# Where a branch is taken, where fetched rows are added, and how a weight row is repeated: three edits in a two-layer encoder kernel

## The chip, the cores and the metric

The kernel runs on one core of a Trainium2 chip. The metric is the device time of one execution in microseconds (us). Three runs of the kernel before gave 1431.76, 1432.56 and 1432.91 us; their median is 1432.56 us.

The names of the engines: PE is TensorE (matrix products; PEld are its weight loads), DVE is VectorE, ACT is ScalarE, POOL is GpSimd, SP is SyncE, which here only issues transfers. Each engine runs its own list of instructions in order; they meet by semaphores.

## The reference

A trunk of two layers over 256 tokens of width 1024, in float32:

```python
h = h + retention_mixer(rms_norm(h, mix_norm[0]), ...)
h = h + swiglu(rms_norm(h, ffn_norm[0]), ...)            # dense
h = h + fourier_mixer(rms_norm(h, mix_norm[1]), ...)
h = h + moe_swiglu(rms_norm(h, ffn_norm[1]), ...)        # top 2 of 8 experts
return rms_norm(h, final_norm)

def moe_swiglu(h, w_router, w_gate, w_up, w_down):
    logits = t @ w_router                                # t: 256 x 1024
    top_val, top_idx = lax.top_k(logits, 2)
    gates = sum(one_hot(top_idx) * softmax(top_val))
    for e in range(8):
        out = out + gates[:, e] * ((silu(t @ w_gate[e]) * (t @ w_up[e])) @ w_down[e])
```

An expert has 1024 x 3584 (gate, up) and 3584 x 1024 (down) weights. With 256 tokens that choose two experts each, an expert gets 64 tokens on average.

## The kernel before, in words

Three stages (retention, dense feed-forward, Fourier mixing) come first; from about 480 us on, the experts run. All three edits lie in the expert stage.

**Precision by splitting.** A float32 operand is split into a high and a low part; a product is the sum of three (`mm3`, lines 248 to 250: whi, wlo and whi again). So each weight tile that lands (`raw`, 1 MB, issued by SP at line 105) is cast to `whi` by ACT (line 131) and reduced to `wlo` by DVE (line 132), each in two halves. Three pairs of `whi`/`wlo` buffers rotate: ACT starts on tile i+2 once PE is through with tile i-1. Eleven `raw` buffers are filled ahead; a buffer is free for the next load when DVE has read it.

**Blocks.** An expert has 7 blocks of 512 hidden columns; there are 56 blocks, counted by `u`. A block is 6 weight tiles of 12 products each on PE: two of the gate, two of the up projection, and two of the down projection of the block before. Between the two gate tiles PE transposes the last block's hidden values (`t4`, line 294, tile `tr<-ident,hm`), which ACT and DVE split into `hth` and `htl` (lines 253 and 254). The hidden values are SiLU of the gate on ACT (line 1107) and its product with up on DVE (line 1111), both as `hm`. At the end of an expert its result goes to a table of rows `back` in DRAM (line 976).

**Small steps between.** A list `work` holds steps that are put between the products: one is taken in the middle of a block (during the first up tile), one at its end. `prep` gathers the tokens of the next two experts. `collect(c)` adds the rows that were fetched for token half c-1 to `X` on DVE (line 904) and then has POOL fetch those of half c by an indirect transfer from `back` (line 909). `final_parts(c)` splits `X` for the last sum (`xf`). `final_gain(hf)` repeats the 1024 final norm weights on all partitions by a product with a row of ones on PE and a copy on ACT (lines 1064 and 1065).

**The overflow branch.** Each expert has 128 slots. If an expert has more tokens, a branch after block 31 (`OVER_AT`) does the rest. The largest count is loaded into a register of each engine (line 1124) and compared (line 1129). In these inputs no expert overflows, so the body is skipped: each engine that has instructions in it jumps over them. The body uses the buffers of the main path (`tr`, two of `mm`, `acc2`, `acc3`), so what comes after the branch waits for the last user of such a buffer inside the body, and gets past when that engine has passed its branch.

The order of the work is written out by hand: instructions stand on each engine in the order in which the program issues them.

Of the kernel before, what the change touches and what calls it, by code (L numbers as in the profile page):

```python
# [11 lines left out]
AF = mybir.ActivationFunctionType  # L12
OP = mybir.AluOpType
PS = bass.MemoryType.PSUM

P = 128
D = 1024
S = 256
# [3 lines left out]
NE = 8  # L22
EPS = 1e-6
HALF = [slice(0, 512), slice(512, 1024)]


def cp(c):
    return slice(c * P, (c + 1) * P)
# [124 lines left out]
def body(nc, tc, a, out, upto=None):  # L153
    with ExitStack() as ctx:
# [6 lines left out]
        te, ve, se, ge = nc.tensor, nc.vector, nc.scalar, nc.gpsimd  # L161
# [53 lines left out]
        gb = gx[:, :D]  # L215
        xgs = [gx[:, D + 512 * i:D + 512 * (i + 1)] for i in range(2)]

        def gain_bcast(ap):
            nc.scalar.dma_start(gb, bcast_rows(ap, D))
# [8 lines left out]
        slot = const.tile([P, P], F32, name="slot")  # L228
        ones = const.tile([P, P], F32, name="ones")
# [11 lines left out]
        def mm(nm="mm"):  # L241
            return ps.tile([P, 512], F32, name=nm, tag="mm", bufs=3)
# [106 lines left out]
        with tc.tile_pool(name="pa", bufs=1) as pa:  # L349
# [43 lines left out]
            p = mm("g8")  # L393
# [171 lines left out]
            q = rope(proj({-1: [second], 0: [first]}, [acc(0), acc(1)]))  # L565
# [8 lines left out]
            q = rope(proj({0: [val(1, 0)], 1: [val(1, 1)], 2: [tg[0].step(0)], 3: [tg[0].step(1)]}))  # L574
# [29 lines left out]
        pt = Aligned(pt_.enter_context(tc.tile_pool(name="pt", bufs=1, side="right")))  # L604
# [4 lines left out]
        with tc.tile_pool(name="pb", bufs=1) as pb:  # L609
# [30 lines left out]
            for u in range(6):  # L640
# [21 lines left out]
                o = dense_h(u)  # L662
# [38 lines left out]
        with tc.tile_pool(name="pc", bufs=1) as pc:  # L701
# [70 lines left out]
            o1, mask, pos, m8 = (const.tile([P, 2, NE], F32, name=n) for n in ("o1", "mask", "pos", "m8"))  # L772
# [65 lines left out]
        with tc.tile_pool(name="pe", bufs=1) as pe, tc.tile_pool(name="dr", bufs=1, space=bass.MemoryType.DRAM) as dr:  # L838
# [61 lines left out]
            def collect(c):  # L900


                for j, t in got:
                    ve.tensor_add(X[:, c - 1], X[:, c - 1], t[:, j])  # L904
                got.clear()
                if c < 2:
                    t = pe.tile([P, 2, D], F32, name="yc", tag="y")
                    for j in range(2):
                        ge.indirect_dma_start(t[:, j], None, back,  # L909
                                              bass.IndirectOffsetOnAxis(at[:, 2 * j + c:2 * j + c + 1], 0))  # L910
                        got.append((j, t))
# [27 lines left out]
            work = list(prep(0))  # L939
            for f in work[:-1]:  # L940
                f()
            work = work[-1:]
# [66 lines left out]
            def overflow(sh, gl, pm, pmr, xe, pt, h, ht, w, gu, tr, y):  # L1009

                for e in range(NE):
                    for c in range(2):
                        ve.tensor_scalar(sh[:, c:c + 1], pos[:, c, e:e + 1], -float(P), None, op0=OP.add)
                        ve.tensor_scalar(pm[:, c], slot, sh[:, c:c + 1], mask[:, c, e:e + 1],
                                         op0=OP.is_equal, op1=OP.mult)
                    ve.tensor_copy(pmr, pm)
                    for q in range(2):
                        o = gu[q]
                        for i in range(4):
                            for c in range(2):  # L1020
                                te.matmul(o[:, cp(i)], nh[:, c, cp(4 * q + i)], pmr[:, c], start=c == 0, stop=False)
                                te.matmul(o[:, cp(i)], nl[:, c, cp(4 * q + i)], pmr[:, c], start=False, stop=c == 1)
                        ve.tensor_copy(xe[:, 4 * q:4 * q + 4], o.rearrange("p (i s) -> p i s", i=4))
                    for c in range(2):
                        te.transpose(tr[:, cp(c)], pm[:, c], ident)
                    ve.tensor_copy(pt, tr[:, :S])
                    for c in range(2):
                        te.matmul(tr[:, :NE + 1], pm[:, c], gts[:, c], start=c == 0, stop=c == 1)
                    ve.tensor_copy(gl, tr[:, :NE + 1])
                    rs, gt = gl[:, NE:], gl[:, e:e + 1]  # L1030
                    for b in range(FE // 512):
                        for o, n in zip(gu, ("moe_w_gate", "moe_w_up")):
                            for s in range(2):
                                wv = w.rearrange("p (k n) -> p k n", k=4)
                                nc.sync.dma_start(wv, cols(a[n][0, e], 512 * b, 512, 4 * s, 4))
                                for k in range(4):
                                    te.matmul(o, xe[:, 4 * s + k], wv[:, k], start=s == 0 and k == 0,
                                              stop=s == 1 and k == 3)
                        se.activation(h, gu[0], AF.Silu, scale=rs)
                        ve.scalar_tensor_tensor(h, gu[1], rs, h, op0=OP.mult, op1=OP.mult)  # L1040
                        for k in range(4):
                            te.transpose(tr[:, cp(k)], h[:, cp(k)], ident)
                        ve.tensor_copy(ht, tr)
                        for s in range(2):
                            wv = w.rearrange("p (k n) -> p k n", k=2)
                            nc.sync.dma_start(wv, cols(a["moe_w_down"][0, e], 0, D, 4 * b + 2 * s, 2))
                            for k in range(2):
                                for hf in range(2):
                                    te.matmul(y[hf], ht[:, cp(2 * s + k)], wv[:, k, HALF[hf]],
                                              start=b == 0 and s == 0 and k == 0,  # L1050
                                              stop=b == 6 and s == 1 and k == 1)
                    for hf in range(2):
                        ve.tensor_scalar(w[:, HALF[hf]], y[hf], gt, None, op0=OP.mult)
                    for c in range(2):
                        for hf in range(2):
                            o = gu[hf]
                            te.matmul(o, pt[:, cp(c)], w[:, HALF[hf]], start=True, stop=True)
                            x = X[:, c, HALF[hf]]
                            ve.tensor_add(x, x, o)

            def final_gain(hf):

                o = mm("gain")
                te.matmul(o, ones[:1], gb[:1, HALF[hf]], start=True, stop=True)  # L1064
                se.copy(gb[:, HALF[hf]], o)

            fin, of = {}, []

# [20 lines left out]
            for u in range(NU):  # L1089
                e, b = divmod(u, 7)  # L1090
                if b == 0 and e % 2 == 1 and e + 1 < NE:
                    work += list(prep(e + 1))
                if u == 2:
                    work.append(rows)
                if b == 1 and e == NE - 1:
                    work[:0] = [lambda c=c: collect(c) for c in range(3)]
                if u == OVER_AT + 3:
                    work += [lambda hf=hf: final_gain(hf) for hf in range(2)]
                if u == NU - 5:
                    work += [lambda c=c: final_parts(c) for c in range(2)]  # L1100
                for s, o in enumerate(moe_h(e)):
                    if s == 0 and u:
                        hidden_t(u - 1)
                    if s == 0 and not u:
                        work.pop(0)()
                hm = pe.tile([P, 512], F32, name="hm")
                se.activation(hm, o, AF.Silu, scale=RS[e])
                for s, o in enumerate(moe_h(e)):
                    if s == 0 and work:
                        work.pop(0)()  # L1110
                ve.scalar_tensor_tensor(hm, o, RS[e], hm, op0=OP.mult, op1=OP.mult)
                hms[u] = hm
                if u == NU - 1:
                    final_start(1)
                if u:
                    moe_down(u - 1, (lambda: hidden_t(NU - 1)) if u == NU - 1 else None)
                if work:
                    work.pop(0)()
                if u == NU - 2:
                    final_start(0)  # L1120
                if u == OVER_AT - 2:
                    counts()
                if u == OVER_AT - 1:
                    most = nc.values_load(cmi[0:1, 0:1])
                    tc.mark_branch_hint_location("over", most > P, engines=[te.engine, ve.engine, nc.sync.engine])
                if u == OVER_AT:
                    nc.scalar.dma_start(gb[:1], a["final_norm"].rearrange("(o d) -> o d", o=1))
                    ov = overflow_tiles()
                    with tc.If(most > P, label="over"):  # L1129
                        overflow(**ov)  # L1130
# [73 lines left out]
```

## Time and profile before

| | before |
|---|---|
| median of 3 runs | 1432.56 us |
| the profiled execution | 1431.94 us, of this the span from first to last instruction 1430.1 us |
| PE busy | 1405.9 us, 98% |
| DVE busy | 1164.9 us, 81% |
| ACT busy | 969.8 us, 68% |
| POOL busy | 70.2 us, 5% |
| mean granted clock of TensorE | 0.995 of full speed |
| transfers | 437.45 MB, in the expert stage about 350 to 390 GB/s |

Times in rows are microseconds from the start of the span. In a row of the timeline the first number is the start, the second the length (of all instructions merged in it; `x4` says how many), and in brackets stands how long the engine sat idle before, and what ended that. `PEq`, `DVEq` and `SPq` are the engines' sequencers, which handle branches and issue transfers.

### The profile page before, as it was taken

What the parts mean: (1) busy time and instruction counts of PE and PEld (TensorE: products, weight loads), DVE (VectorE), ACT (ScalarE), POOL (GpSimd) and SP (SyncE); (2) the same over time, 40 slices, a digit from 0 to 9 for tenths busy, and PEclk for the clock granted to TensorE, in tenths of its full rate; (3) what the DMA queues carried; (4) which work ended last, traced back from release to release, by engine and by line L of the source; (5) the groups of instructions that cost most, each with busy time, mean ns of one, the idle gap of its engine ahead of it and who ended that gap; (6) DMA issues with size and microseconds to landing.
All of it is one profiled execution on the core that took longest, in us unless ns stands there. A gap on an engine that the chain in (4) does not pass through costs nothing. (4 is left out here: it accounts for less than half of the span.)

```text
span 1430.1 us, 17313 instructions
## 1 busy us (share of the span) xinstructions
PE 1405.9 (98%) x6533; PEld 1166.7 (82%) x6533; DVE 1164.9 (81%) x1201; ACT 969.8 (68%) x1120; POOL 70.2 (5%) x109
## 2 busy tenths in 40 slices
PE   7999999999999999999999999999999999999997
PEld 6888878888888888888888888887878888888786
DVE  6866666545577999989999988998988898999996
ACT  5544446444455777777877777787777778778775
POOL 8400000000001000000000000000000000001000
PEclk9999999999999999999999999999999999999999
DMA  8646539755536989999999999999999999999990
GB/s 288 213 154 205 177 132 375 251 179 200 181 120 243 385 302 358 371 356 340 334 394 393 386 361 364 362 347 390 348 373 361 356 373 366 393 383 346 395 347 30
DMA packets 186700, 437.45 MB, mean 306 GB/s; under 512 B 8161, under 2 KB 10993, under 8 KB 186610
## 3 DMA queue, kind: packets, MB, share of 16 engines
q1 hardware_dynamic: 181424, 426.27, 81.7%
q10 hardware_dynamic: 4610, 7.92, 1.5%
q0 software_dynamic: 576, 2.10, 0.4%
q8 instruction: 52, 0.85, 0.2%
q14 instruction: 38, 0.31, 0.1%
HBM read 431.54 MB, written 4.72 MB: 305 GB/s over the span
## 5 line engine op out<-in xcount | busy, mean ns | idle before, releaser
L132 DVE TENSOR_TENSOR wlo<-raw,whi 128x1024 fp32r<-128x1024 f32 (+1 forms) x789 | 923.5, 1219 | 148.3 <-ACT whi L131 139.9
L131 ACT CAST whi<-raw 128x1024 fp32r<-128x1024 f32 (+1 forms) x789 | 786.1, 1047 | 200.7 <-PE acc L250 106.3
L248 PE MATMUL mm<-whi,xe 128*128 128x512 f32 x896 | 355.1, 396 | 0.3 <-PEq L1129 0.3
L250 PE MATMUL mm<-whi,xe 128*128 128x512 f32 x896 | 349.6, 390 | 0.0
L249 PE MATMUL mm<-wlo,xe 128*128 128x512 f32 x896 | 349.2, 390 | 0.0
L249 PE MATMUL acc<-wlo,hth 128*128 128x512 f32 x528 | 206.3, 391 | 2.3 <-DVE wlo L132 2.3
L248 PE MATMUL acc<-whi,hth 128*128 128x512 f32 x528 | 206.2, 391 | 0.0
L250 PE MATMUL acc<-whi,htl 128*128 128x512 f32 x528 | 206.1, 390 | 0.0
L250 PEld LDWEIGHTS mm<-whi,xe 128*128 128x128 f32 x896 | 168.2, 188 | 36.1
L248 PEld LDWEIGHTS mm<-whi,xe 128*128 128x128 f32 x896 | 168.4, 188 | 34.9 <-issue 2.2
L249 PEld LDWEIGHTS mm<-wlo,xe 128*128 128x128 f32 x896 | 168.5, 188 | 32.9
L248 PE MATMUL mm<-whi,nhi 128*128 128x512 f32 (+1 forms) x352 | 135.6, 385 | 0.0
L250 PE MATMUL mm<-whi,nlo 128*128 128x512 f32 (+1 forms) x352 | 133.9, 380 | 0.0
L249 PE MATMUL mm<-wlo,nhi 128*128 128x512 f32 (+1 forms) x352 | 133.7, 380 | 0.0
L249 PEld LDWEIGHTS acc<-wlo,hth 128*128 128x128 f32 x528 | 99.5, 188 | 23.3 <-DVE wlo L132 2.8
L250 PEld LDWEIGHTS acc<-whi,htl 128*128 128x128 f32 x528 | 99.5, 188 | 20.7
L248 PEld LDWEIGHTS acc<-whi,hth 128*128 128x128 f32 x528 | 99.6, 189 | 20.6
L253 ACT CAST hth<-tr 128x512 fp32r<-128x512 f32 (+1 forms) x67 | 38.9, 581 | 84.8 <-PE tr L294 84.8
L250 PEld LDWEIGHTS mm<-whi,nlo 128*128 128x128 f32 x352 | 66.2, 188 | 12.9
L249 PEld LDWEIGHTS mm<-wlo,nhi 128*128 128x128 f32 x352 | 66.3, 188 | 11.8
L248 PEld LDWEIGHTS mm<-whi,nhi 128*128 128x128 f32 x352 | 66.3, 188 | 11.9
L254 DVE TENSOR_TENSOR htl<-tr,hth 128x512 fp32r<-128x512 f32 (+1 forms) x67 | 45.7, 682 | 33.5 <-ACT hth L253 33.5
(291 smaller groups left out, 992.6 us busy)
## 6 DMA issues: line engine op xcount, KB each, us to landing
raw<-in_moe_w_gate SPq DMA_DIRECT2D x110, 1024.0 KB, 7.6
raw<-in_moe_w_down SPq DMA_DIRECT2D x108, 1024.0 KB, 7.6
raw<-in_moe_w_up SPq DMA_DIRECT2D x105, 1024.0 KB, 7.3
raw<-in_ret_w_in SPq DMA_DIRECT2D x23, 1024.0 KB, 5.2
raw<-in_dense_w_gate SPq DMA_DIRECT2D x11, 1024.0 KB, 5.3
raw<-in_dense_w_up SPq DMA_DIRECT2D x11, 1024.0 KB, 8.8
raw<-in_dense_w_down SPq DMA_DIRECT2D x11, 1024.0 KB, 6.6
raw<-in_ret_w_out SPq DMA_DIRECT2D x8, 1024.0 KB, 4.9
```

The source lines that it names most:

```text
L131: self.nc.scalar.copy(hi[sl], t[sl])
L132: self.nc.vector.tensor_sub(lo[sl], t[sl], hi[sl].bitcast(F32))
L248: te.matmul(o, lh, rh, start=first, stop=False)
L249: te.matmul(o, lh, rl, start=False, stop=False)
L250: te.matmul(o, ll, rh, start=False, stop=last)
L253: se.copy(hi, src)
L254: ve.tensor_sub(lo, src, hi.bitcast(F32))
```

## The change

There are three parts.

1. The body of the overflow branch uses no DVE. What DVE did there is done by ACT (copies, casts and scalings) and POOL (the choice of slots, products of two tiles, the additions to `X`). The hint that names the engines of the branch lists ACT in place of DVE.
2. `collect(0)`, `collect(1)` and `collect(2)` are put in the list at blocks 50, 51 and 52 (b = 1, 2 and 3 of the last expert); all three were put there at block 50.
3. The final norm's weights are read by one transfer that repeats the row on all 128 partitions (`gain_bcast`, 512 KB, issued by ACT at block 34). Before, 4 KB were loaded just before the branch, and `final_gain` did the rest at block 34.

```diff
                 for e in range(NE):
                     for c in range(2):
-                        ve.tensor_scalar(sh[:, c:c + 1], pos[:, c, e:e + 1], -float(P), None, op0=OP.add)
-                        ve.tensor_scalar(pm[:, c], slot, sh[:, c:c + 1], mask[:, c, e:e + 1],
+                        ge.tensor_scalar(sh[:, c:c + 1], pos[:, c, e:e + 1], -float(P), None, op0=OP.add)
+                        ge.tensor_scalar(pm[:, c], slot, sh[:, c:c + 1], mask[:, c, e:e + 1],
                                          op0=OP.is_equal, op1=OP.mult)
-                    ve.tensor_copy(pmr, pm)
+                    se.copy(pmr, pm)
...
-                    ve.tensor_copy(pt, tr[:, :S])
+                    se.copy(pt, tr[:, :S])
...
-                    ve.tensor_copy(gl, tr[:, :NE + 1])
+                    se.copy(gl, tr[:, :NE + 1])
...
                         se.activation(h, gu[0], AF.Silu, scale=rs)
-                        ve.scalar_tensor_tensor(h, gu[1], rs, h, op0=OP.mult, op1=OP.mult)
+                        se.activation(ht, gu[1], AF.Copy, scale=rs)
+                        ge.tensor_mul(h, h, ht)
...
-                        ve.tensor_copy(ht, tr)
+                        se.copy(ht, tr)
...
                             te.matmul(o, pt[:, cp(c)], w[:, HALF[hf]], start=True, stop=True)
+                            se.copy(h, o)
                             x = X[:, c, HALF[hf]]
-                            ve.tensor_add(x, x, o)
-
-            def final_gain(hf):
-
-                o = mm("gain")
-                te.matmul(o, ones[:1], gb[:1, HALF[hf]], start=True, stop=True)
-                se.copy(gb[:, HALF[hf]], o)
+                            ge.tensor_add(x, x, h)
...
-                if b == 1 and e == NE - 1:
-                    work[:0] = [lambda c=c: collect(c) for c in range(3)]
+                if 1 <= b <= 3 and e == NE - 1:
+                    work[:0] = [lambda c=b - 1: collect(c)]
                 if u == OVER_AT + 3:
-                    work += [lambda hf=hf: final_gain(hf) for hf in range(2)]
+                    work.append(lambda: gain_bcast(a["final_norm"]))
...
-                    tc.mark_branch_hint_location("over", most > P, engines=[te.engine, ve.engine, nc.sync.engine])
+                    tc.mark_branch_hint_location("over", most > P, engines=[te.engine, se.engine, nc.sync.engine])
                 if u == OVER_AT:
-                    nc.scalar.dma_start(gb[:1], a["final_norm"].rearrange("(o d) -> o d", o=1))
```

ACT's list at the branch, before: four weight tiles are cast in eight halves, the 4 KB transfer is issued, and the jump goes over 56 activations.

```order
320 L1107 ACTIVATE hm<-mm,gl 128x512
321 L131 CAST whi<-raw 128x1024 x8
322 L1127 DMA gx<-in_final_norm 1x1024
323 L1129 COMPARE_AND_BRANCH
324 L1039 ACTIVATE ov_xe<-mm,ov_ogl 128x512 x56
325 L1129 UNCONDITIONAL_BRANCH x2
326 L131 CAST whi<-raw 128x1024 x2
```

The same place on ACT after the change (the tiles of the body are named `ov_`):

```order
322 L1103 ACTIVATE hm<-mm,gl 128x512
323 L131 CAST whi<-raw 128x1024 x8
324 L1124 COMPARE_AND_BRANCH
325 L1016 CAST ov_pmr<-ov_pm 128x256
326 L1023 COPY ov_xe<-mm 128x512 x2
327 L1026 COPY ov_pt<-tr 128x256
328 L1029 COPY ov_ogl<-tr 128x9
```

The casts stand where they stood; the jump now goes over 256 instructions. On DVE it went over 232 and now goes over none; on POOL it goes over 49, and over none before; PE's 1321 and SP's 336 are as many as they were.

DVE's list in the last expert, before. The additions of fetched rows are `X<-X,yc`; `wlo` are halves of weight tiles, `hm` and `htl` the hidden values, `xf` the split of `X`:

```order
702 L132 TENSOR_TENSOR wlo<-raw,whi 128x1024 x4
703 L904 TENSOR_TENSOR X<-X,yc 128x1024 x2
704 L132 TENSOR_TENSOR wlo<-raw,whi 128x1024 x2
705 L254 TENSOR_TENSOR htl<-tr,hth 128x512
706 L132 TENSOR_TENSOR wlo<-raw,whi 128x1024 x4
707 L904 TENSOR_TENSOR X<-X,yc 128x1024 x2
708 L132 TENSOR_TENSOR wlo<-raw,whi 128x1024 x2
```

The same list after the change:

```order
502 L132 TENSOR_TENSOR wlo<-raw,whi 128x1024 x4
503 L904 TENSOR_TENSOR X<-X,yc 128x1024 x2
504 L132 TENSOR_TENSOR wlo<-raw,whi 128x1024 x2
505 L1107 SCALAR_TENSOR_TENSOR hm<-mm,gl,hm 128x512
506 L132 TENSOR_TENSOR wlo<-raw,whi 128x1024 x4
507 L254 TENSOR_TENSOR xf<-X,xf 128x512 x2
508 L132 TENSOR_TENSOR wlo<-raw,whi 128x1024 x2
509 L254 TENSOR_TENSOR htl<-tr,hth 128x512
510 L132 TENSOR_TENSOR wlo<-raw,whi 128x1024 x4
511 L904 TENSOR_TENSOR X<-X,yc 128x1024 x2
512 L132 TENSOR_TENSOR wlo<-raw,whi 128x1024 x2
```

Between the two pairs of additions there were 6 halves of weight tiles, and there are 12 now, a whole block; the first two `xf` splits, which stood behind both pairs, now stand between them.

## Rows read from the trace of the kernel before

**Rows 1.** The page: busy time of each engine.
```profile
PE 1405.9 (98%) x6533; PEld 1166.7 (82%) x6533; DVE 1164.9 (81%) x1201; ACT 969.8 (68%) x1120; POOL 70.2 (5%) x109
```
**Rows 2.** Timeline of PE, the transposes of hidden values, one group a block.
```profile
980.24 0.60 PE L294 MATMUL tr<-ident,hm 128*128 128x128 f32 x4
999.73 0.63 PE L294 MATMUL tr<-ident,hm 128*128 128x128 f32 x4 [1.96 <-DVEq L1129]
...
1033.34 0.60 PE L294 MATMUL tr<-ident,hm 128*128 128x128 f32 x4
1052.70 0.60 PE L294 MATMUL tr<-ident,hm 128*128 128x128 f32 x4
...
1309.81 0.60 PE L294 MATMUL tr<-ident,hm 128*128 128x128 f32 x4
1326.62 0.60 PE L294 MATMUL tr<-ident,hm 128*128 128x128 f32 x4
1347.67 0.60 PE L294 MATMUL tr<-ident,hm 128*128 128x128 f32 x4
```
**Rows 3.** Waits of SP over the span: us in total, times, longest.
```profile
SPq L105 <- DVE wlo L132: 1062.5, 358, 26.6
...
SPq L1129 <- SPq L1129: 8.5, 2, 5.6
```
**Rows 4.** Waits of the other engines over the span, the one for landing weights.
```profile
ACT whi L131 <- DMA raw<-in_ret_w_in: 5.5, 2, 4.4
```
**Rows 5.** Transfers by line: KB each, median us from issue to landing.
```profile
raw<-in_moe_w_down SPq DMA_DIRECT2D x108, 1024.0 KB, 7.6
...
yc<-back,at POOLq DMA_INDIRECT x4, 8.7
```
**Rows 6.** Timeline of PE, the last product before the wait behind the branch.
```profile
997.39 0.39 PE L250 MATMUL mm<-whi,xe 128*128 128x512 f32 x1
```
**Rows 7.** Timeline of DVE at the branch.
```profile
990.50 4.74 DVE L132 TENSOR_TENSOR wlo<-raw,whi 128x1024 fp32r<-128x1024 f32 x4
999.75 2.36 DVE L132 TENSOR_TENSOR wlo<-raw,whi 128x1024 fp32r<-128x1024 f32 x2 [4.51 <-DVEq L1129]
```
**Rows 8.** Timeline of ACT at the branch.
```profile
991.80 0.49 ACTq L1127 DMA_DIRECT2D gx<-in_final_norm  x1
992.75 1.05 ACT L131 CAST whi<-raw 128x1024 fp32r<-128x1024 f32 x1
994.51 2.00 ACT L131 CAST whi<-raw 128x1024 fp32r<-128x1024 f32 x2 [0.71 <-PE acc L250]
```
**Rows 9.** The products that repeat the weights: min/median/max ns, first and last start.
```profile
L1064 PE MATMUL gain<-gx,ones x4: 587/640/692, 1039.4 to 1049.3; 1*128 1x512 f32 x4
```
**Rows 10.** Timeline of DVE around the additions of fetched rows.
```profile
1309.51 2.36 DVE L132 TENSOR_TENSOR wlo<-raw,whi 128x1024 fp32r<-128x1024 f32 x2 [1.51 <-ACT whi L131]
...
1324.74 2.48 DVE L904 TENSOR_TENSOR X<-X,yc 128x1024 f32<-128x1024 f32 x2
...
1330.01 4.62 DVE L132 TENSOR_TENSOR wlo<-raw,whi 128x1024 fp32r<-128x1024 f32 x4
1335.79 1.23 DVE L904 TENSOR_TENSOR X<-X,yc 128x1024 f32<-128x1024 f32 x1 [1.16 <-DMA yc<-back,at]
...
1339.43 2.35 DVE L132 TENSOR_TENSOR wlo<-raw,whi 128x1024 fp32r<-128x1024 f32 x2
...
1346.90 1.29 DVE L254 TENSOR_TENSOR xf<-X,xf 128x512 fp32r<-128x512 f32 x2
```
**Rows 11.** Timeline of PE in the same place.
```profile
1337.97 0.39 PE L248 MATMUL acc<-whi,hth 128*128 128x512 f32 x1
1340.70 0.76 PE L249 MATMUL acc<-wlo,hth 128*128 128x512 f32 x1 [2.35 <-DVE wlo L132]
```
**Rows 12.** Windows behind both waits: busy us (x), granted clock (PEclk), DMA share, GB/s.
```profile
1340.70:1344.00 3.30, 3.30 (x8) 2.62 (x9) 3.30 (x4) 0.70 (x2) 0.00 (x0) 0.51 1.05 386
...
999.70:1003.00 3.30, 3.27 (x17) 2.82 (x18) 3.25 (x4) 2.49 (x3) 0.00 (x0) 1.00 1.03 402
```

More of the change, by code (lines that the diff above doesn't have):

```diff
@@ L1022, in overflow @@
                                 te.matmul(o[:, cp(i)], nl[:, c, cp(4 * q + i)], pmr[:, c], start=False, stop=c == 1)
-                        ve.tensor_copy(xe[:, 4 * q:4 * q + 4], o.rearrange("p (i s) -> p i s", i=4))
+                        se.copy(xe[:, 4 * q:4 * q + 4], o.rearrange("p (i s) -> p i s", i=4))
                     for c in range(2):
                         te.transpose(tr[:, cp(c)], pm[:, c], ident)
-                    ve.tensor_copy(pt, tr[:, :S])
+                    se.copy(pt, tr[:, :S])
                     for c in range(2):
                         te.matmul(tr[:, :NE + 1], pm[:, c], gts[:, c], start=c == 0, stop=c == 1)
-                    ve.tensor_copy(gl, tr[:, :NE + 1])
+                    se.copy(gl, tr[:, :NE + 1])
                     rs, gt = gl[:, NE:], gl[:, e:e + 1]
@@ L1052, in overflow @@
                     for hf in range(2):
-                        ve.tensor_scalar(w[:, HALF[hf]], y[hf], gt, None, op0=OP.mult)
+                        se.activation(w[:, HALF[hf]], y[hf], AF.Copy, scale=gt)
                     for c in range(2):
```

## The prediction, made before the changed kernel ran

> **What bounds the kernel now.** I read the page first: PE is busy for 98% of the span, DVE for 81%, ACT for 68% [rows 1]. Then I looked for a beat. In the expert stage PE transposes the last block's hidden values once a block, so the distance of two such rows is the time of a block. Where nothing disturbs, it is 16.81 us (1309.81 to 1326.62) [rows 2]: 72 products and 4 short transposes with no gap, 0.23 us for each. There only PE counts, and what holds PE up for a microsecond makes the end a microsecond later. Three blocks of the stretch that the change touches are longer [rows 2]:
>
> - 980.24 to 999.73: 19.49, so 2.68 too long. The branch lies in it.
> - 1033.34 to 1052.70: 19.36, so 2.55 too long. The products that repeat the norm's weights lie in it.
> - 1326.62 to 1347.67: 21.05, so 4.24 too long. The fetched rows are added in it.
>
> Together 9.47 us: that is all the change can win. Transfers are not the bound. SP waited 1062.5 us in all for DVE to free a buffer, the longest of these waits 26.6 us [rows 3], and ACT waited for a landing weight tile only in the first stage [rows 4]. The reader is to see in this that loads wait for room, not work for loads: a block takes 6 MB in 16.81 us (374 GB/s, from sizes), a tile lands 7.6 us after its issue [rows 5], while eleven buffers at 2.8 us a tile are a lead of some 30 us.
>
> **The branch.** PE's last product before the long wait starts at 997.39 [rows 6]; the transposes would follow 0.23 later, at 997.62, and start at 999.73: a wait of 2.11. The remaining 0.57 of the 2.68 is PE's own jump and a slightly slower start behind it; that stays. The wait is for DVE: it ended its last split at 995.24 (990.50 + 4.74) and began the next at 999.75, 4.51 later, and in that time its sequencer was at the branch [rows 7]. `tr`, the transposes' buffer, has its last user inside the body on DVE, so PE can't go on until DVE is past it. ACT passed its own branch meanwhile: the next cast starts at 994.51, only 0.71 behind the cast before, and waits there for PE, not for the branch [rows 8]. The difference between the two is what is jumped over: 232 instructions on DVE, 56 on ACT.
>
> After the change DVE jumps over nothing and ACT over 256. So ACT takes over the stall, I assume, and `tr` is now released by ACT. What it costs is decided by when ACT gets there. ACT ends its last cast before the branch at 993.80 (992.75 + 1.05) [rows 8], 1.44 before DVE ended its own. With DVE's 4.51 it is past at 998.31, and PE waits 0.69 in place of 2.11: 1.42 saved. Counted instead from the moment an engine's sequencer reaches the branch, ACT is earlier still, since the 4 KB transfer right ahead of the branch is issued at 991.80 [rows 8]; then nothing is left of the wait and 2.11 is saved. I take 1.5, close to the row with the duration. The bad end is a stall as long as SP's, 8.5 us at its branch [rows 3], though SP has landing transfers to wait for there: ACT past at 1002.30, PE waiting 4.68, so 2.6 lost. Behind ACT's branch stand the casts of the next weight tile; they end 2 us after it, at about 1000.3, and PE needs that tile's low part one wait (0.69), four transposes (0.44) and twelve products (2.73) after 997.62, at 1001.5, so DVE still has time for it.
>
> [...]
>
> POOL's jump over 49 hides nothing: POOL is 5% busy [rows 1] and nobody waits for it here.
>
> **The weights of the final norm.** Four products of 0.6 us each and two restarts go from PE [rows 9], and two copies from ACT: the whole 2.55. Added is one transfer of 512 KB. ACT issues it; the issue took 0.49 for the 4 KB one [rows 8], on an engine with a third of its time idle; it waits there for the weight tile whose cast is next in any case, so nothing new is queued behind it. Its volume is 1.4 us of the block's 374 GB/s; the lead of the weight loads hides that, and without a lead the saving would be 2.55 - 1.4 = 1.15. I take 2.55.
>
> **The fetched rows.** Before, the second pair of additions waited for the second fetch, which was issued only when the first pair was done; such a fetch takes 8.7 us to land [rows 5]. DVE was free at 1334.63 (1330.01 + 4.62) and got to the next weight half at 1339.43, 4.80 late [rows 10]. PE wanted its low part at 1338.20 and got it at 1340.70: 2.50 late [rows 11]. So DVE may be 2.30 late at that place. The first pair, at 1324.74, had put it back by 2.4, of which one block's idle time, 1.51 [rows 10], had made good all but 0.9; from being on time DVE may be 3.2 late. [...]
>
> After the change a whole block lies between the pairs, more than the 8.7 us of a fetch, so no addition waits for a transfer. But DVE gets within one block 2.4 of additions, 1.2 of splits of `X` (1.29 for the two, overlapped) and 2.4 of additions again [rows 10]: 6.0, less one block's idle 1.5, is 4.5 late where 3.2 is covered. PE waits 1.3; with a tenth for the tiles behind it, 1.4 is left of 4.24, and 2.8 saved. The first pair alone (2.4) is covered. A wait of 1.4 is shorter than the one at the branch that left the clock alone, so I add nothing for the clock. [...]
>
> **The sum.** 1.5 + 2.55 + 2.8 = 6.85. The profiled execution takes 1431.94 (span 1430.1); after the change 1425.1. It lies 0.6 below the median of the runs, 1432.56, so the median after is 1425.7.
>
> **The rivals.**
>
> - The pile on DVE costs as much as the fetch did: additions and splits together, the wait long enough to halve the clock. For it: DVE is 91% busy in a block (15.3 of 16.81) and 4.5 late is not far from 4.8. Against: the first pair cost PE nothing. The time is 1432.56 - 1.5 - 2.55 - 0.2 = 1428.3.
> - ACT pays more at its jump than DVE did, or DVE's stall is not one of jumping and stays. For it: ACT stands ahead of DVE in every weight tile. Against: ACT's free passage before. The branch's term is between 0 and -2.6: 1427.2 to 1429.8.
> - All waits go: 2.11 + 2.55 + 4.24 = 8.9, so 1423.7. For it: the 1.51 is one gap of one block, and four halves take 4.62 us in one place and 4.74 in another [rows 7, 10], so that a block's 12 halves may be 0.4 shorter than I count. Against: two pairs and a split within one block.
> - Slower: transfers are the bound from the branch on, since their share there is 1.03 to 1.05 [rows 12]. Then PE's waits are only time in which loads catch up, taking them away returns nothing, and the 512 KB cost 1.4: 1434.0. It decides only once a tile lands later than the 30 us of lead; against it stand 7.6 us to landing [rows 5] and SP's waits for room [rows 3].
>
> **How the numbers follow.** The forecast with its own spread (1424.5 to 1427) gets 0.60, the pile on DVE 0.13, the dearer jump 0.12, all waits gone 0.11, slower 0.02, and 0.02 that two of the bad cases meet. The range of 8 in 10 is 1423.3 to 1429.0. A difference under 0.2%, 2.9 us, can't be told from none in this kernel: within it lie times over 1429.7, which only the end of the dear jump, two bad cases together, or the bound of transfers give: 0.07 the same, 0.02 slower (over 1435.4), 0.91 faster.
>
> **What will show it.** On DVE, no idle time at the branch; on ACT, some 4.5 us between the last cast before and the first behind it, and PE's transposes waiting for ACT by 0 to 0.7 us, a block of 17.4 to 18.1. No `gain` rows, and the block at 1033 to 1050 back at 16.81. In the last expert no addition that waits for a fetch, and one wait of PE for `wlo` of 1 to 1.5 us behind the second pair, with the granted clock at 1.00 behind it. I am wrong if PE's wait at the branch is not shorter, if the clock falls in the last expert, or if ACT is seen waiting for `raw`.

## The result, and the profile after

| | before | after |
|---|---|---|
| median, lowest to highest, of 4 runs each | 1432.52 us (1431.76 to 1432.91) | 1424.41 us (1424.06 to 1424.62) |
| profiled execution (span) | 1431.94 us (1430.1) | 1424.62 us (1422.8) |
| mean granted clock | 0.995 | 0.997 |

The ratio of after to before is 0.9948, with a 95% interval of 0.9936 to 0.996. So the change is faster by 0.5%: 8.1 us by the medians, 7.3 by the two profiled executions.

The page's busy times, which answer to [rows 1]. They hardly moved: PE lost 3.7 us of work, the other engines less than 1.5. The rest of what was won is PE's idle time.

```profile
PE 1402.2 (99%) x6529; PEld 1165.5 (82%) x6529; DVE 1164.3 (82%) x1201; ACT 968.5 (68%) x1118; POOL 70.1 (5%) x109
```

The beat, PE's transposes in the timeline, as in [rows 2]. (980.35 to 997.74 is the block with the branch, 1031.34 to 1048.15 the one that had the norm's products, 1338.87 to 1357.11 the one with the second pair of additions.)

```profile
980.35 0.60 PE L294 MATMUL tr<-ident,hm 128*128 128x128 f32 x4
997.74 0.60 PE L294 MATMUL tr<-ident,hm 128*128 128x128 f32 x4
...
1031.34 0.60 PE L294 MATMUL tr<-ident,hm 128*128 128x128 f32 x4
1048.15 0.60 PE L294 MATMUL tr<-ident,hm 128*128 128x128 f32 x4
...
1322.07 0.60 PE L294 MATMUL tr<-ident,hm 128*128 128x128 f32 x4
1338.87 0.60 PE L294 MATMUL tr<-ident,hm 128*128 128x128 f32 x4
1357.11 0.60 PE L294 MATMUL tr<-ident,hm 128*128 128x128 f32 x4
```

The differences are 17.39, 16.81 and 18.24 where 19.49, 19.36 and 21.05 stood: 2.10, 2.55 and 2.81 won, 7.46 together. The profiled executions differ by 7.32, so the three blocks hold the whole gain. Of the bracket behind 999.73 in [rows 2] nothing is left at 997.74: PE no longer waits for its transposes' buffer.

The branch itself: DVE's timeline, which answers to [rows 7].

```profile
990.61 4.74 DVE L132 TENSOR_TENSOR wlo<-raw,whi 128x1024 fp32r<-128x1024 f32 x4
998.69 2.36 DVE L132 TENSOR_TENSOR wlo<-raw,whi 128x1024 fp32r<-128x1024 f32 x2 [3.34 <-ACT whi L131]
```

ACT's timeline, which answers to [rows 8], and ACT's branch itself with the first instruction of its sequencer behind it (the times of these two are starts, the lengths in front are ns).

```profile
991.90 2.01 ACT L131 CAST whi<-raw 128x1024 fp32r<-128x1024 f32 x2 [0.72 <-PE acc L250]
997.60 2.00 ACT L131 CAST whi<-raw 128x1024 fp32r<-128x1024 f32 x2 [3.69 <-ACTq L1124]
...
L1124 ACTq COMPARE_BRANCH  x1: 76/76/76, 991.9 to 991.9; - x1
L1124 ACTq EVENT_SEMAPHORE  x1: 17/17/17, 997.4 to 997.4; - x1
```

DVE is still idle for 3.34, but its releaser is now ACT's cast: it waits for data, not at a branch. The stall has moved to ACT, whose sequencer (ACTq) is named. ACT's sequencer is past at 997.4, and PE starts its transposes at 997.74 without a bracket: the stall fits in by 0.3 at most.

The last expert, DVE's timeline, which answers to [rows 10]: both pairs of additions are single rows of two with no bracket, so neither waits for a transfer, and the second (1347.88) comes a block after the first (1329.40).

```profile
1329.40 2.48 DVE L904 TENSOR_TENSOR X<-X,yc 128x1024 f32<-128x1024 f32 x2
...
1339.26 1.28 DVE L254 TENSOR_TENSOR xf<-X,xf 128x512 fp32r<-128x512 f32 x2
...
1347.88 2.48 DVE L904 TENSOR_TENSOR X<-X,yc 128x1024 f32<-128x1024 f32 x2
1350.27 2.36 DVE L132 TENSOR_TENSOR wlo<-raw,whi 128x1024 fp32r<-128x1024 f32 x2
```

PE's timeline in the same place, which answers to [rows 11].

```profile
1350.23 0.39 PE L248 MATMUL acc<-whi,hth 128*128 128x512 f32 x1
1351.55 0.50 PE L249 MATMUL acc<-wlo,hth 128*128 128x512 f32 x1 [0.93 <-DVE wlo L132]
1351.88 0.39 PE L250 MATMUL acc<-whi,htl 128*128 128x512 f32 x1
1352.11 0.40 PE L248 MATMUL acc<-whi,hth 128*128 128x512 f32 x1
...
1354.17 0.39 PE L248 MATMUL mm<-whi,xe 128*128 128x512 f32 x1
1354.48 0.50 PE L249 MATMUL mm<-wlo,xe 128*128 128x512 f32 x1
1354.81 0.40 PE L250 MATMUL mm<-whi,xe 128*128 128x512 f32 x1
```

A product would follow its neighbour by 0.23; the one at 1351.55 comes 1.32 behind, so it is 1.09 late. The products behind the wait follow each other by 0.33 once and then by 0.23, and the next tile is late by another 0.08 (0.31 at 1354.48). With the two restarts (0.10 each) that makes 1.37 of the 1.43 by which the block is still too long. The window behind the wait (its length; the busy us of PE, PEld, DVE, ACT and POOL with their instructions; granted clock; DMA share; GB/s), which answers to the first row of [rows 12], has the full clock:

```profile
1351.55:1354.40 2.85, 2.85 (x12) 2.17 (x12) 2.85 (x4) 1.95 (x4) 0.00 (x0) 1.00 1.05 386
```

### The profile page after: what moved, and what is told of

Same layout as the page of the kernel before. It is cut to its first block, busy times and chain, and to the rows that moved or that the text cites. A ratio compares the mean times of both kernels' runs of the same rounds, so it can differ in the third digit from the quotient of the medians.

```text
span 1422.8 us, 17302 instructions
## 1 busy us (share of the span) xinstructions
PE 1402.2 (99%) x6529; PEld 1165.5 (82%) x6529; DVE 1164.3 (82%) x1201; ACT 968.5 (68%) x1118; POOL 70.1 (5%) x109
```

## The experiments

### Each part by itself

Three kernels are the kernel before with one part of the diff each: `p1_branch` part 1 (all lines of the body and the hint), `p2_collect` part 2, `p3_gain` part 3. The single lines that tell them apart:

```diff
# p1_branch, beside the body's operations (on se and ge in place of ve)
-                    tc.mark_branch_hint_location("over", most > P, engines=[te.engine, ve.engine, nc.sync.engine])
+                    tc.mark_branch_hint_location("over", most > P, engines=[te.engine, se.engine, nc.sync.engine])
# p2_collect
-    if b == 1 and e == NE - 1:
-        work[:0] = [lambda c=c: collect(c) for c in range(3)]
+    if 1 <= b <= 3 and e == NE - 1:
+        work[:0] = [lambda c=b - 1: collect(c)]
# p3_gain
-        work += [lambda hf=hf: final_gain(hf) for hf in range(2)]
+        work.append(lambda: gain_bcast(a["final_norm"]))
...
-        nc.scalar.dma_start(gb[:1], a["final_norm"].rearrange("(o d) -> o d", o=1))
```

Expected of `p1_branch`:

> The kernel before with part 1 alone (overflow body without DVE). Theory: only DVE's stall at the jump held PE's transposes there, and ACT reaches its branch early enough; the block with the branch goes from 19.49 to about 17.4 us, nothing else changes: 1432.5 - 2.1 = 1430.4 us. Rival: the stall only moves to ACT and PE loses the same later in the block, as ACT is ahead of DVE for each weight tile: 1432.5 us.

Expected of `p2_collect`:

> The kernel before with part 2 alone (the fetched rows' steps a block apart). Theory: no addition waits for a fetch, the clock stays, PE waits 1 to 1.4 us once for the pile of additions and splits on DVE: the long block goes from 21.05 to about 18.2, 1432.5 - 2.8 = 1429.7 us. Rival: the pile on DVE costs what the fetch did and halves the clock: 1432.3 us.

Expected of `p3_gain`:

> The kernel before with part 3 alone (the norm's weights repeated by a transfer). Theory: the products' 2.55 us go and the 512 KB are hidden: 1432.5 - 2.55 = 1430.0 us, the block at 1033 us 16.81 long. Rival: the transfer delays weight loads that PE needs: 1.4 us of it come back, 1431.3 us, with ACT seen waiting for landing weights.

Measured on one chip, against 1431.93 us of before there:

| part alone | median us (lowest to highest, 11 runs) | ratio and interval | length of its block |
|---|---|---|---|
| 1, branch | 1429.56 (1428.61 to 1430.17) | 0.9982, 0.9973 to 0.9991 | 17.45 |
| 2, fetched rows | 1429.14 (1428.5 to 1431.6) | 0.9985, 0.9976 to 0.9994 | 18.24 |
| 3, norm weights | 1428.28 (1427.89 to 1430.2) | 0.9977, 0.9968 to 0.9986 | 16.81 |

Each part shortens its own block. By the medians part 1 gives 2.37, part 2 2.79 and part 3 3.65 us, where 2.1, 2.8 and 2.55 were expected; with intervals of some 1.3 us to either side, none of the differences is clear of noise. The three gains add up to 8.8 us, over the 7.3 to 8.1 that all three give together, and this too is within noise. But the blocks, read from one execution each, show that something is counted twice: with part 1 or part 3 alone the additions are as before, and yet the block that holds them became shorter. PE's timeline there, with part 1 alone:

```profile
1339.43 0.50 PE L249 MATMUL acc<-wlo,hth 128*128 128x512 f32 x1 [2.27 <-DVE wlo L132]
...
1345.00 0.60 PE L294 MATMUL tr<-ident,hm 128*128 128x128 f32 x4
1362.28 0.60 PE L294 MATMUL tr<-ident,hm 128*128 128x128 f32 x4
```

With part 3 alone, the window behind the wait of 2.41 us that stands there:

```profile
1337.83:1341.00 3.17, 3.17 (x13) 2.42 (x14) 3.17 (x4) 0.96 (x3) 0.00 (x0) 1.00 1.06 388
```

The waits are as long as the 2.35 of [rows 11], but the clock stayed at 1.00, with 13 products in 3.17 us (the same with part 1, from 1339.43 on), where [rows 12] have 0.51 and 8 in 3.30. The block is 19.57 long with part 1 and 19.75 with part 3, in place of 21.05. Then the next one is 0.4 to 0.5 too long (17.28 and 17.25, where before had 16.81), as if DVE were still behind there and PE, at a full clock, ran up against it. Together 3.23 and 3.38 too long, in place of 4.24. So by these two kernels the low clock cost about 0.9 to 1.0 net, an estimate, not the 1.74 that PE's lateness of 2.50 [rows 11] leaves of the 4.24.

### The kernel before once more

No edit; it tells whether the low clock behind that wait belongs to the kernel or to one execution.

> The kernel before, unchanged, profiled once more. Question: is the lowered clock behind PE's wait in the last expert a property of this kernel or of one execution? [...] If it belongs to the kernel (rival), the block between the transposes around 1327 and 1348 is again 20.8 to 21.3 long, with products 0.4 apart behind a wait of 2.3 to 2.4. If it varies from execution to execution (theory, from the kernels with part 1 or part 3 alone), the block is about 19.6 to 19.8, products 0.23 apart, and the next block some 0.4 too long. The branch block is 19.4 to 19.5 and the one with the norm's weights 19.3 to 19.4 under both. Time 1431 to 1433.

It took 1431.56 us (one run). PE's wait, and the window of [rows 12], which here starts 0.19 behind the wait's end:

```profile
1340.51 0.79 PE L249 MATMUL acc<-wlo,hth 128*128 128x512 f32 x1 [2.45 <-DVE wlo L132]
```

```profile
1340.70:1344.00 3.30, 3.30 (x9) 2.60 (x10) 3.30 (x4) 0.40 (x1) 0.00 (x0) 0.56 1.05 385
```

The rival was right: the low clock came back (0.56, a block of 20.98), so in this kernel it was there in both profiled executions. With part 1 or part 3 alone, a wait of the same length left the clock alone, in one profiled execution each. What decides it is not the length of this wait alone; what else does stays open, and so does whether these two kernels always keep the clock.

### How far the jump goes

`short_body` is the kernel before with an overflow body for 2 of the 8 experts (the body would be incomplete if an expert overflowed; none does). DVE then jumps over 58 instructions in place of 232.

```diff
-                for e in range(NE):
+                for e in range(2):
```

> The kernel before with the overflow body for 2 of the 8 experts only (the rest of the overflow is left out; it isn't executed in these inputs): DVE jumps over 58 instructions in place of 232, as ACT did over 56. Theory: the stall comes from the distance jumped. DVE's idle time at the branch falls from 4.5 to under 1 us, PE doesn't wait at the transposes, the block is 17.4 long. [...]

DVE's timeline at the branch:

```profile
991.74 4.74 DVE L132 TENSOR_TENSOR wlo<-raw,whi 128x1024 fp32r<-128x1024 f32 x4
996.82 2.36 DVE L132 TENSOR_TENSOR wlo<-raw,whi 128x1024 fp32r<-128x1024 f32 x2 [0.35 <-ACT whi L131]
```

The stall of 4.51 in [rows 7] is gone; the 0.35 that is left is a wait for ACT's cast. The block is 17.39, as after the change. The engine and the kind of its operations are the same, so the stall goes with the long body: 4.51 at a jump over 232 instructions, none at 58. (A shorter body also moves the place in the code to which the jump goes; no run tells these two apart.) The time, 1432.71 us, hardly shows it (1433.76 for before on that chip, one run each), because in this execution the fetches landed later (the second pair of additions waited 2.47 and 1.58 for them, 1.16 and 1.27 in the kernel before) and the block of the additions was 22.71 long. PE's wait there, and the window behind it:

```profile
1341.45 0.50 PE L249 MATMUL acc<-wlo,hth 128*128 128x512 f32 x1 [3.96 <-DVE wlo L132]
...
1341.45:1344.75 3.30, 3.30 (x10) 2.67 (x11) 3.30 (x4) 0.00 (x0) 0.00 (x0) 0.69 1.05 387
```

The clock fell here too, so a part of the 22.71 is its doing.

### From when the stall counts

`act_op` is the changed kernel with one copy of 1 us more on ACT, right before the branch (it writes into a tile whose content is no longer needed). If the stall starts when ACT has done its work, ACT gets past 1 us later. If it starts when ACT's sequencer, which runs ahead of the work (after the change it is at the branch at 991.9, and ACT casts until 993.91), comes to the branch, nothing moves.

```diff
                 if u == OVER_AT:
+                    se.copy(gx[:, D:], gx[:, :D])
                     ov = overflow_tiles()
```

> The changed kernel with one more copy of 128x1024 (1.05 us) on ACT right before its branch. Theory: the stall runs from when ACT's sequencer reaches the branch, which is ahead of its work; the copy only fills the stall: idle 2.7 in place of 3.7, resumed as before 5.6 us after the start of the last pair of casts, block 17.4. Rival: the stall runs from the end of ACT's last work; ACT resumes 1 us later and PE waits 0.9 us: 18.3.

ACT's timeline:

```profile
992.59 2.01 ACT L131 CAST whi<-raw 128x1024 fp32r<-128x1024 f32 x2 [0.72 <-PE acc L250]
994.50 1.04 ACT L1123 COPY gx<-gx 128x1024 f32<-128x1024 f32 x1
998.18 1.05 ACT L131 CAST whi<-raw 128x1024 fp32r<-128x1024 f32 x1 [2.64 <-DMA raw<-in_moe_w_down]
```

ACT goes on 5.59 after the start of the last pair of casts, after the change without the copy 5.70 (991.90 to 997.60). The copy took its time out of the idle time, 2.64 in place of 3.69, and the block stayed at 17.38. So the stall counts from when the sequencer gets to the branch, here at the start of the last casts, and of its length that much is hidden for which the engine still has work.

The rows of the branch itself say the same: here of ACT in `act_op`, and of DVE in the kernel before.

```profile
L1125 ACTq COMPARE_BRANCH  x1: 76/76/76, 992.6 to 992.6; - x1
L1125 ACTq EVENT_SEMAPHORE  x1: 17/17/17, 998.0 to 998.0; - x1
...
L1129 DVEq COMPARE_BRANCH  x1: 84/84/84, 993.8 to 993.8; - x1
L1129 DVEq EVENT_SEMAPHORE  x1: 21/21/21, 999.6 to 999.6; - x1
```

From the branch to the sequencer's next instruction it is 5.4 on ACT with the copy, 5.5 without it, and 5.8 on DVE: nearly one price for both engines. DVE's 4.51 of idle time were what its work left over of it.

In this trace and in that of `no_hint` below, the row names a landing of `w_down` as what ended ACT's wait, in place of ACTq. ACT did not wait for weights there: in `no_hint` the transfer that is named was issued at 990.10 and landed at 999.42, after the cast had begun, and the tile that is cast, issued at 968.18, had landed at 978.11.

With part 1 alone, where ACT's sequencer first issues the 4 KB transfer, it was 5.98 (992.59 to 998.57), later by somewhat less than that issue, and the block was 17.45:

```profile
992.59 1.06 ACT L131 CAST whi<-raw 128x1024 fp32r<-128x1024 f32 x1 [0.71 <-PE acc L250]
992.60 0.50 ACTq L1129 DMA_DIRECT2D gx<-in_final_norm  x1
...
998.57 1.05 ACT L131 CAST whi<-raw 128x1024 fp32r<-128x1024 f32 x1 [3.97 <-ACTq L1131]
```

The execution with the copy took 1425.3 us.

### What the hints do

`no_hint` is the changed kernel without ACT in the list of the hint, `no_pe_hint` the same without PE.

```diff
# no_hint
-                    tc.mark_branch_hint_location("over", most > P, engines=[te.engine, se.engine, nc.sync.engine])
+                    tc.mark_branch_hint_location("over", most > P, engines=[te.engine, nc.sync.engine])
# no_pe_hint
-                    tc.mark_branch_hint_location("over", most > P, engines=[te.engine, se.engine, nc.sync.engine])
+                    tc.mark_branch_hint_location("over", most > P, engines=[se.engine, nc.sync.engine])
```

> The changed kernel without ACT in the branch's hint. Theory: the hint brought ACT nothing, as DVE stalled 4.5 us with it; ACT resumes some 5.6 us after the start of its last pair of casts (3.7 idle), the block stays at 17.4. Rival: the hint shortens ACT's stall; without it ACT resumes 1 us later or more, and PE waits for it: 18.4 or longer.

> The changed kernel without PE in the branch's hint; PE jumps over 1321 instructions. [...]

ACT's timeline without its hint:

```profile
991.94 2.00 ACT L131 CAST whi<-raw 128x1024 fp32r<-128x1024 f32 x2 [0.71 <-PE acc L250]
997.60 2.00 ACT L131 CAST whi<-raw 128x1024 fp32r<-128x1024 f32 x2 [3.65 <-DMA raw<-in_moe_w_down]
```

PE's timeline without PE's hint, with the row of PE's branch (its sequencer's rows stand under `PEldq`), and behind it the same two after the change, with the hint:

```profile
993.95 0.39 PE L250 MATMUL acc<-whi,htl 128*128 128x512 f32 x1
996.91 0.47 PE L248 MATMUL mm<-whi,xe 128*128 128x512 f32 x1 [2.57 <-PEq L1124]
...
L1124 PEldq COMPARE_BRANCH  x1: 6402/6402/6402, 990.1 to 990.1; - x1
```

```profile
994.88 0.47 PE L248 MATMUL mm<-whi,xe 128*128 128x512 f32 x1 [0.30 <-PEq L1124]
...
L1124 PEldq COMPARE_BRANCH  x1: 383/383/383, 990.4 to 990.4; - x1
```

ACT's hint brings nothing (3.65 idle without, 3.69 with; 1424.64 us). PE's takes the branch from 6.40 us to 0.38; as work still queued hides much of that, PE itself gains 2.27 (2.57 idle without, 0.30 with). The time follows: 1426.6 us, 2.0 above the profiled execution after, the block at 19.65. I had expected a block of 21, which was too long; the direction was right. Why the hint works on PE and not on ACT is not shown. Each is one execution, but the idle times are read from the place itself.

### The steps one to a block

`spread` is the changed kernel with the five steps of the last expert in five blocks; after the change the first two splits of `X` came in the block between the two pairs of additions.

```diff
-                if 1 <= b <= 3 and e == NE - 1:
-                    work[:0] = [lambda c=b - 1: collect(c)]
+                if e == NE - 1 and 1 <= b <= 5:
+                    work.append([lambda: collect(0), lambda: collect(1), lambda: final_parts(0),
+                                 lambda: collect(2), lambda: final_parts(1)][b - 1])
...
-                if u == NU - 5:
-                    work += [lambda c=c: final_parts(c) for c in range(2)]
```

> The changed kernel with one step of the last sum in each of five blocks: fetch, add and fetch, split of X, add, split of X. Theory: PE's last wait in the last expert comes from two pairs of additions and a split on DVE within one block; with one of them a block (2.4 us against 3.2 covered) the wait of 1.4 us goes: 1424.4 - 1.4 = 1423.0 us, all blocks of the last expert 16.81 long. Rival: a pair of additions alone is enough to make PE wait in this place: 1424.4 us or two smaller waits.

It was timed again later, beside the changed kernel on one chip:

> The changed kernel, unchanged, timed beside the one with a step per block on one chip. Time 1424.3 to 1424.7, ratio to before 0.9945 to 0.9952; collect block again 18.2 to 18.3, branch block 17.4.

> The changed kernel with the last expert's steps one to a block, timed beside the changed kernel on one chip. Theory (the 1.43 that the collect block is still too long are DVE being late, and come back when the steps are apart): 1.2 to 1.5 us below the changed kernel, its largest time below the other's smallest. Rival (the earlier difference of 1.2 was between two chips): 0 to 0.4 apart.

| | median us (lowest to highest, 5 runs) | ratio to before and interval |
|---|---|---|
| `spread` | 1423.23 (1422.78 to 1423.7) | 0.9942, 0.9928 to 0.9955 |
| `after_again` | 1424.54 (1424.01 to 1425.51) | 0.9947, 0.9933 to 0.9961 |
| `spread_again` | 1422.9 (1422.54 to 1423.86) | 0.9938, 0.9925 to 0.9952 |

PE's transposes in `spread_again`: the blocks of the last expert up to 1371.90 have 16.8 each.

```profile
1338.29 0.60 PE L294 MATMUL tr<-ident,hm 128*128 128x128 f32 x4
1355.10 0.60 PE L294 MATMUL tr<-ident,hm 128*128 128x128 f32 x4
1371.90 0.60 PE L294 MATMUL tr<-ident,hm 128*128 128x128 f32 x4
```

The 1.43 that the change left behind is won too. On one chip the medians lie 1.64 apart, and the slowest run of `spread_again` is below the fastest of `after_again`, whose blocks were 17.39 (branch) and 18.28 (additions), as after the change. `spread` is the fastest of the kernels, and shows that what PE still waited for was DVE being late by two additions and a split within one block.

## Why the prediction was right, point by point

**The beat.** Right. PE's blocks explain the time: 7.46 us in three blocks, 7.32 between the profiled executions.

**The branch: mechanism right, term too small (1.5; measured 2.10).** ACT did take over DVE's stall: 3.69 idle, ACTq named, 256 instructions jumped over. `short_body` shows that the stall goes with the long body (4.51 of idle time at 232 instructions; at 58 only 0.35, a wait for ACT's cast), and `no_hint` that the hint doesn't remove the stall on ACT (3.65 without it, 3.69 with it). So jumps over 56 (ACT before, whose next cast waited 0.71 for PE [rows 8]) and 58 instructions went without a stall on these two engines, those over 232 and 256 with one; at what length it begins no run shows. On PE the jump over 1321 is not free by itself: without its hint the branch took 6.40, of which PE was idle for 2.57, and with it 0.38.

The step that failed was the choice between two counts. I added DVE's 4.51 of idle time to the end of ACT's work (998.31) and took a sum near that, 1.5. Idle time is the stall less the work that still hides it (on DVE 5.8 less some 1.4, from its branch at 993.8 to the end of its work at 995.24), so it can't be carried over from one engine to another: `act_op` shows that the stall runs from where the sequencer reaches the branch (the copy of 1.04 only took its time out of ACT's idle time, 2.64 for 3.69). The other count of the prediction, by which nothing is left of the wait (2.11), was the right one. The bad end was misread as well: the 8.5 of SP in [rows 3] are two waits, the longest 5.6. (Nor is SP's wait shown to be one of the jump: in `short_body`, where SP jumps over a quarter as much, it is 5.8 from its branch to its next instruction, and 5.6 before.) The 0.57 that I left as PE's own share stayed: 0.58.

**The norm's weights.** Right: 2.55 forecast, 2.55 measured in the block, 3.65 with part 3 alone by the medians, of which the clock of another block is a part (the block of the additions: 19.75 for 21.05, at 1.00 for 0.51). The 512 KB cost nothing that shows; their issue is one short row on ACT's queue in that block:

```profile
1034.86 0.36 ACTq L219 DMA_DIRECT2D gx<-in_final_norm  x1
```

**The fetched rows: right in sum, one step of it wrong.** Forecast were 1.4 left and 2.8 won, measured 1.43 and 2.81. No addition waits for a fetch, PE has one wait of note (1.09) behind the second pair, the clock is 1.00, and `spread` confirms that the rest was DVE being late. What failed is the split of the 4.24: the 1.74 that PE's lateness of 2.50 leaves of it I put to the clock of 0.51 [rows 12] as a plain addition, and no run shows that. By the kernels with part 1 or part 3 alone the wait would have cost 3.2 to 3.4 over two blocks at a full clock, so the clock's share is about 0.9 to 1.0; that DVE caught up while PE was slow fits this, but is not shown by itself. And "a wait of 1.4 is shorter than the one that left the clock alone" was no sound reason: waits of 2.27 and 2.41 left it alone too. The forecast did not suffer, because it was counted from DVE's lateness and not from the clock.

**The sum.** The forecast for the profiled execution was 1425.1, and it took 1424.62: 0.6 more from the branch, 0.1 less elsewhere. The forecast median, 1425.7, is 1.3 above the measured 1424.41: those 0.5, then 0.6 that I added because the profiled execution of before lay below its median, while that of after lies 0.2 above its own.

**The rivals.** The pile on DVE at the old price fell (1.43 left, clock full). A dearer jump fell (no wait left at the branch). "All waits gone" did not happen, as 1.43 was left in the last expert, though its 1423.7 lies nearer to the measured median than my 1425.7; `spread` then got below it by putting the steps elsewhere (1422.9). The bound by transfers fell: ACT waits for no landing weight tile in the last expert, and SP's waits for room are as long as before [rows 3]:

```profile
SPq L105 <- DVE wlo L132: 1057.3, 360, 26.6
```

**The signs.** One of them failed: DVE did have idle time at the branch, 3.34, as it waits there for ACT's cast, which ACT's stall delays. On ACT 3.69 lie between the casts, not some 4.5, for the reason given under the branch. The others came as forecast.

## What to carry to other kernels

When one engine works without a gap in a steady beat, measure that beat: each block's excess over it is what a change there can win, and here the excesses added up to the gain. A branch that jumped far (256 instructions on ACT, 232 on DVE) cost the jumping engine a stall of 5.4 to 5.8 us here, from the moment its sequencer arrived, so put the far jump on an engine that still has work queued there, or that nobody waits for until the stall is over. Where side work is fitted into a nearly full engine, count its lateness block by block and give each step a block of its own.

## What the runs showed of the hardware that was not expected

- A far jump took 5.4 to 5.8 us from the branch to the sequencer's next instruction, on ACT (256 instructions) and DVE (232); on ACT it made no difference whether the work queued ahead of it was 2.0 us or 3.0 us long (`act_op`).
- A hint on the branch took PE's own branch from 6.40 us to 0.38 at a jump over 1321 instructions, of which PE gained 2.27, and brought ACT nothing at one over 256 (3.65 us of idle time without it, 3.69 with it).
- The granted clock fell to about half (0.51, 0.56) behind a wait of 2.35 and 2.45 us of PE in the kernel before, and fell behind one of 3.96 us in `short_body` (0.69 in the window behind it). It stayed at 1.00 behind waits of 2.27 and 2.41 us at the same place in two kernels that differ from before elsewhere. Why was not settled.
